# Row broadcasts of two heads in turn, and the first norm's sums from token-major squares

## The chip, the core and the metric

The kernel runs on one core of one Trainium2 chip, in one launch. The metric is the device time of an execution in microseconds (us), smaller is better. The core has a matrix engine (TensorE, PE in the profile, with its weight loads as PEld), VectorE (DVE), ScalarE (ACT), GpSimd (POOL) and a sync engine (SP) that issues most loads. Each engine runs its own instructions in order and waits on semaphores for the others.

## The reference

Two transformer blocks follow each other on 512 tokens of 1024 features, all in float32. Cut to what matters here:

```python
def first_block(x, ...):
    h = rmsnorm(x, norm1_g)                    # x * rsqrt(mean(x*x) + eps) * g, per token
    q, k, v, cb, cc, cx, g_attn, g_conv = split(h @ w_in)
    q, k = partial_rope(rmsnorm(q)), partial_rope(rmsnorm(k))     # per head of 64
    attn = windowed_gqa(q, k, v, sink)         # softmax over a window, 8 heads, 2 kv heads
    x = x + (sigmoid(g_attn) * (attn @ w_ap) + sigmoid(g_conv) * (conv @ w_cp)) @ w_out
    return x + hierarchical_moe(rmsnorm(x, norm2_g), ...)
def second_block(x, ...):
    # layer 0: two full attentions of 8 heads each ("a", and "b" from latents), then an MLP
    # layer 1: neighbourhood attention of 16 heads, then an MLP; a last norm
```

In each attention the output of a head is divided, per token, by the sum of its exponentials. In each norm the features are multiplied, per token, by the reciprocal root of the mean square.

## The kernel before

Activations lie feature-major: a tile has 128 features on the partitions and the 512 tokens along the row, and `x` is eight such tiles. Float32 products are made of three matmuls on split operands (`mm3`, L226 to L228: high by high, high by low, low by high), each of 512 tokens. Weights arrive in a ring of three buffers (`raw`, L103), are split by ScalarE (`wh`, L124) and VectorE (`wl`, L133) three groups ahead of their use, and a product of 8 blocks (24 matmuls) fills one of two accumulators (`psacc`).

The order of the instructions is written by generators. `run` steps a main generator, one quantum for each block of three matmuls, and lets a side generator (an attention) step in between; `later(n, f)` calls `f` after n quanta. So a number in `later` sets where in each engine's order an instruction stands, and not when it runs.

The start (`window`) loads `x` as `xin`, splits it into H and L, and makes products at once; the norm's factor is applied behind them. The first 16 quanta make the first two products block by block in turn; the third to sixth follow, 8 quanta each. `Heads.take` evicts each of the first five on ScalarE twice, scaled (`z`, L567) and squared (L568), and lets TensorE sum the squares per head four quanta on (`psO`, L300); the rotary part takes a shuffle on VectorE (L576), two multiplications on GpSimd (L577, L578) and an addition on VectorE (L582), and `write_q` casts the result on ScalarE (L640, L642). The sixth product is V (L626, transposed at L631).

The first norm's sum of squares is made beside this: `square` takes the eight tiles of `xin` in turns on ScalarE (L351, L357) and VectorE (L355), GpSimd adds them up in `ss` (L364), `norm_tokens` sums over the partitions with four matmuls (psT, L300), VectorE makes the factor `rcol` per token (L319 to L289), and `rows` broadcasts it along the partitions (`rstd`, L326, L333).

A row broadcast turns a column of 128 token values into a row that is the same on all partitions: the matmul takes the column, repeated, as the weights and the identity as the moving operand. Where two heads of 64 features share a tile, head 0 fills partitions 0 to 63 of the result and head 1 partitions 64 to 127, with 64 output columns each. This stands in `scale_k` (L611, the factor of k) and in `f_step` (L719, the reciprocal sums `rs` of the two heads of a unit; ScalarE copies the result to `rb`, L721). There are 4 units in the window attention, 4 and 4 in layer 0, and 8 in layer 1, where `GridPV` has its own `rows` with five pieces, the last of 64 tokens (L1410).

## Time and profile before

| | us |
| --- | --- |
| median of 3 runs | 1891.06 (1889.78 to 1893.31) |
| the profiled execution | 1888.91 |
| its span, first to last instruction | 1887.1 |
| TensorE busy in the span | 1824.1 |
| VectorE busy | 1080.7 |
| ScalarE busy | 724.4 |
| GpSimd busy | 342.3 |

The profile is of one execution. A matmul on float32 operands shows as two passes, and matmuls are pipelined, so the busy time of an engine is that in which at least one instruction was in flight. The stages by time: the window block to about 290 us, routing and experts to about 640, layer 0 to about 1320 with its attentions between 690 and 900, layer 1 from there with its attention between 1320 and 1500, then the last MLP. The clock of a row is the share of TensorE's full clock of 2.4 GHz that was granted on average over the stretch; the two levels are 1.2 and 2.4 GHz.

### The profile page before, as it was taken

Reading aid. Unit: us, or ns where it says so; the run is one execution under the profiler, and the core shown is the slowest. Engines: PE = TensorE matmul, PEld = TensorE weight load, DVE = VectorE, ACT = ScalarE, POOL = GpSimd, SP = SyncE. Lnnn points to the kernel's source line nnn. Section 1 sums busy time; section 2 is a strip of 40 time slices with the busy share of each in tenths; the row PEclk is TensorE's granted clock in tenths of the full one; section 3 lists DMA queues with packets and bytes.
Section 4 is the critical chain, followed back from the end, with each engine's and each line's share of the span. In section 5 each row is a group of like instructions: output and inputs, shape, how many; then the busy total and the mean of one; then the engine's idle time right before and its main releaser. Section 6 shows DMA issues by size and latency. Waiting matters only on the chain.

```text
span 1887.1 us, 23667 instructions
## 1 busy us (share of the span) xinstructions
PE 1824.1 (97%) x8890; PEld 1369.5 (73%) x8890; DVE 1080.7 (57%) x1956; ACT 724.4 (38%) x1418; POOL 342.3 (18%) x356
## 2 busy tenths in 40 slices
PE   7999999799999899999999999999999999999998
PEld 6777787534444686667888888878777788888887
DVE  7765447534433767765655555563766565555555
ACT  4444334211111456654433333333555443333334
POOL 5310003110000251001211111121443221111111
PEclk9999999899999999999999999999999999999999
DMA  5211336599999220302222222233222232322321
GB/s 189 77 51 68 131 131 252 183 359 417 422 419 403 88 95 18 84 29 84 101 101 89 102 100 89 102 128 117 79 57 57 90 112 90 107 95 90 107 94 45
DMA packets 67334, 257.08 MB, mean 136 GB/s; under 512 B 22224, under 2 KB 28752, under 8 KB 42128
## 3 DMA queue, kind: packets, MB, share of 16 engines
q1 hardware_dynamic: 54848, 227.41, 32.6%
q0 software_dynamic: 5712, 19.66, 3.2%
q10 hardware_dynamic: 6656, 8.45, 1.3%
q8 instruction: 72, 1.18, 0.3%
q14 instruction: 46, 0.38, 0.1%
HBM read 245.28 MB, written 8.39 MB: 134 GB/s over the span
## 4 chain that ended last, share of the span: by engine, by line
PE 56%; DVE 6%; ACT 2%; issue 1%; DMA 0%; POOL 0%; POOLq 0%; DVEq 0%; ACTq 0%
PE psacc L226 15%; PE psacc L228 15%; PE psacc L227 14%; PE psT L695 2%; PE psO L849 2%; DVE wl L133 1%; PE psT L326 1%; PE psO L1418 1%; PE psT L1410 1%; PE psS L1475 1%; PE psS L226 1%; PE psS L1159 1%; PE psS L227 1%; PE psS L228 1%; ACT p L682 1%
## 5 line engine op out<-in xcount | busy, mean ns | idle before, releaser
L133 DVE TENSOR_TENSOR wl<-raw,wh 128x512 fp32r<-128x512 f32 x466 | 403.3, 869 | 245.8 <-ACT wh L124 241.8
L226 PE MATMUL psacc<-xh,wh 128*128 128x512 f32 x1008 | 408.9, 406 | 7.0 <-ACT wh L124 6.4
L124 ACT CAST wh<-raw 128x512 fp32r<-128x512 f32 x466 | 285.8, 617 | 323.4 <-PE psacc L227 273.6
L227 PE MATMUL psacc<-xl,wh 128*128 128x512 f32 x1008 | 395.6, 392 | 1.2 <-DVE xl L250 1.2
L228 PE MATMUL psacc<-xh,wl 128*128 128x512 f32 x1008 | 395.9, 393 | 0.1
L226 PEld LDWEIGHTS psacc<-xh,wh 128*128 128x128 f32 x1008 | 190.9, 189 | 56.4 <-issue 14.2
L228 PEld LDWEIGHTS psacc<-xh,wl 128*128 128x128 f32 x1008 | 190.4, 189 | 41.9 <-DVE wl L133 0.6
L227 PEld LDWEIGHTS psacc<-xl,wh 128*128 128x128 f32 x1008 | 191.2, 190 | 35.4 <-DVE xl L250 2.5
L226 PE MATMUL psacc<-uh,wh 128*128 128x512 f32 x480 | 187.0, 390 | 2.6 <-DVE x L438 2.6
L228 PE MATMUL psacc<-uh,wl 128*128 128x512 f32 x480 | 186.8, 389 | 0.0
L227 PE MATMUL psacc<-ul,wh 128*128 128x512 f32 x480 | 186.7, 389 | 0.0
L406 POOL TENSOR_TENSOR t<-t,rstd 128x512 f32<-128x512 f32 x64 | 83.1, 1299 | 526.4 <-ACT t L405 526.4
L438 DVE TENSOR_TENSOR x<-psacc,x 128x512 f32<-128x512 f32 x120 | 82.7, 689 | 125.4 <-PE psacc L228 125.4
L364 POOL TENSOR_TENSOR ss<-ss,t 128x512 f32<-128x512 f32 (+1 forms) x56 | 69.6, 1242 | 262.0 <-ACT t L357 241.4
L226 PEld LDWEIGHTS psacc<-uh,wh 128*128 128x128 f32 x480 | 90.1, 188 | 22.3 <-issue 3.7
L228 PEld LDWEIGHTS psacc<-uh,wl 128*128 128x128 f32 x480 | 90.1, 188 | 18.9
L227 PEld LDWEIGHTS psacc<-ul,wh 128*128 128x128 f32 x480 | 90.1, 188 | 18.6
L242 ACT CAST uh<-t 128x512 fp32r<-128x512 f32 x64 | 39.7, 620 | 131.4 <-DVE t L407 131.4
L695 PE MATMUL psT<-cst,p 128*128 128x128 f32 x448 | 77.1, 277 | 13.1 <-ACT p L682 12.8
L695 PEld LDWEIGHTS psT<-cst,p 128*128 128x128 f32 x448 | 55.2, 140 | 42.4 <-ACT p L682 22.7
L405 ACT ACTIVATE t<-psacc 128x512 f32<-128x512 f32 x64 | 38.2, 597 | 80.7 <-PE psacc L228 80.7
L703 DVE COPY pt<-psT 128x256 f32<-128x256 f32 (+1 forms) x80 | 43.2, 540 | 39.4 <-PE psT L695 38.7
(461 smaller groups left out, 2786.1 us busy)
## 6 DMA issues: line engine op xcount, KB each, us to landing
raw<-ffn SPq DMA_DIRECT2D x64, 1024.0 KB, 4.8
ew<-e_w SPq DMA_DIRECT2D x15, 2048.0 KB, 11.2
raw<-e_w SPq DMA_DIRECT2D x20, 1024.0 KB, 10.0
esH<-e_w SPq DMA_DIRECT2D x8, 2048.0 KB, 12.8
esL<-e_w SPq DMA_DIRECT2D x8, 2048.0 KB, 12.5
raw<-w_in_a SPq DMA_DIRECT2D x8, 1024.0 KB, 4.8
raw<-od_qk SPq DMA_DIRECT2D x8, 1024.0 KB, 4.7
raw<-w_gccp SPq DMA_DIRECT2D x8, 768.0 KB, 4.1
```

The costliest lines, as they stand in the source:

```text
L124: nc.scalar.copy(h[:, :n], r)
L133: self.nc.vector.tensor_sub(l, r, h)
L226: nc.tensor.matmul(acc, wh, xh, start=first, stop=False)
L227: nc.tensor.matmul(acc, wh, xl, start=False, stop=False)
L228: nc.tensor.matmul(acc, wl, xh, start=False, stop=last)
L242: nc.scalar.copy(h, src)
L364: self.nc.gpsimd.tensor_add(s, s, q)
L405: nc.scalar.activation(r, acc, AF.Relu)
L406: nc.gpsimd.tensor_mul(r2, r, st["r2"])
L438: nc.vector.tensor_add(X[:, d], acc, X[:, d])
L695: nc.tensor.transpose(t[:, o:o + 128], p[:, m * 128:m * 128 + 128], c.ident)
L703: nc.vector.tensor_copy(dst, src)
```

## The change

First, `pair_rows` takes the place of the two calls of `rows` in `scale_k` and `f_step`: for each block of tokens it issues the matmul of head 0 and then that of head 1, and not all blocks of head 0 first. The five pieces of `GridPV` become a table that `pair_rows` reads. The matmuls themselves are the same.

Second, the first norm's sums come from another copy of `x`. The host lays out `xN`, with the tokens on the partitions (128 partitions, four tokens each, 1024 features a token). Three loads on SP's queue, behind the masks of the attention and ahead of the next weights, bring it into the three buffers `pt0` to `pt2`, which the attention uses only later. ScalarE squares eight pieces of 512 in place and sums each along the row (`accum_out`) into a column of `sq`. VectorE adds the two columns of a token, and the factor follows as before. The squares stand at quanta 25 to 39, where those of `xin` stood at 10 to 31; `stats` moves from 24 to 27 and `rows` from 31 to 33 quanta behind the second product. The squares of `xin`, the additions on GpSimd and the four matmuls over `ss` are gone.

```diff
-    def rows(self, cols, t, p0=0, p1=128):
+    def rows(self, cols, t):
...
+    def pair_rows(self, cols, t, pieces=None):
...
+        for i, o, a, n in pieces or [(i, i * 128, 0, 128) for i in range(cols.shape[1])]:
+            for h in range(2):
+                self.nc.tensor.matmul(t[64 * h:64 * h + 64, o:o + n], cols[:, i, h:h + 1].to_broadcast([128, 64]),
+                                      self.ident[:, a:a + n], start=True, stop=True)
...
-            for h in range(2):
-                c.rows(f[:, :, h], t, 64 * h, 64 * h + 64)
+            c.pair_rows(f, t)
...
-        for hh in range(2):
-            pv.rows(d["rs"][:, :, hh], t, 64 * hh, 64 * hh + 64)
+        c.pair_rows(d["rs"], t, pv.pieces)
...
-        c.later(10 + 3 * d, lambda d=d: c.square(s, xin[:, d], d, d % 2))
...
+    sq = pool.tile([128, 8], F32, name="sq")
+    for i, r in enumerate(room):
+        n = min(1536, 4096 - 1536 * i)
+        r = r.rearrange("p a b -> p (a b)")
+        nc.sync.dma_start(r[:, :n], a["xN"][:, 1536 * i:1536 * i + n])
+        for j in range(n // 512):
+            x, o = r[:, 512 * j:512 * j + 512], sq[:, 3 * i + j:3 * i + j + 1]
+            c.later(25 + 2 * (3 * i + j), lambda x=x, o=o: nc.scalar.activation(x, x, AF.Square, accum_out=o))
...
-        st["rcol"] = c.norm_tokens(s)
+        s4 = c.few((4,))
+        nc.vector.tensor_add(s4, sq[:, 0::2], sq[:, 1::2])
+        st["rcol"] = c.rstd(s4, 4, D)
...
-                c.later(24, stats)
-                c.later(31, rows)
+                c.later(27, stats)
+                c.later(33, rows)
```

How the order on GpSimd changes, from its first operation on 512 tokens to the start of the factors' chain; before:

```order
L364 TENSOR_TENSOR ss_90<-ss_90,t_219 128x512
L364 TENSOR_TENSOR ss_90<-ss_90,t_232 128x512
L577 TENSOR_TENSOR t_256<-z_235,wcos_152 128x512
L578 TENSOR_TENSOR t_257<-t_257,wsin_153 128x512
L577 TENSOR_TENSOR t_261<-z_239,wcos_152 128x512
L578 TENSOR_TENSOR t_262<-t_262,wsin_153 128x512
L364 TENSOR_TENSOR ss_90<-ss_90,t_269 128x512
L364 TENSOR_TENSOR ss_90<-ss_90,t_293 128x512
L364 TENSOR_TENSOR ss_90<-ss_90,t_316 128x512
L577 TENSOR_TENSOR t_325<-z_305,wcos_152 128x512
L578 TENSOR_TENSOR t_326<-t_326,wsin_153 128x512
```

and now (`z` are the evicted products, two multiplications for each):

```order
L591 TENSOR_TENSOR t_252<-z_231,wcos_151 128x512
L592 TENSOR_TENSOR t_253<-t_253,wsin_152 128x512
L591 TENSOR_TENSOR t_257<-z_235,wcos_151 128x512
L592 TENSOR_TENSOR t_258<-t_258,wsin_152 128x512
L591 TENSOR_TENSOR t_313<-z_295,wcos_151 128x512
L592 TENSOR_TENSOR t_314<-t_314,wsin_152 128x512
```

The additions into `ss` are gone, and the multiplications of the next product follow at once.

On ScalarE, from the square of the third product (its eviction `psacc`) to the weight cast behind the eviction of the fourth; before:

```order
L568 ACTIVATE t_306<-psacc_243 128x512
L124 CAST wh_310<-raw_113 128x512
L642 CAST qst_146<-z_239 64x512
L357 ACTIVATE t_336<-xin_91 128x512
L124 CAST wh_344<-raw_113 128x512
L640 CAST qst_146<-z_305 64x512
L567 ACTIVATE z_365<-psacc_309,gains_80 128x512
L568 ACTIVATE t_366<-psacc_309 128x512
L124 CAST wh_370<-raw_113 128x512
```

and now (`pt0` and `pt1` hold the copy of `x`):

```order
L582 ACTIVATE t_296<-psacc_239 128x512
L124 CAST wh_300<-raw_112 128x512
L908 ACTIVATE pt0_158,sq_161<-pt0_158 128x512
L655 CAST qst_145<-z_235 64x512
L908 ACTIVATE pt0_158,sq_161<-pt0_158 128x512
L124 CAST wh_330<-raw_112 128x512
L908 ACTIVATE pt0_158,sq_161<-pt0_158 128x512
L908 ACTIVATE pt1_159,sq_161<-pt1_159 128x512
L653 CAST qst_145<-z_295 64x512
L581 ACTIVATE z_350<-psacc_299,gains_80 128x512
L582 ACTIVATE t_351<-psacc_299 128x512
L124 CAST wh_355<-raw_112 128x512
```

One square of `xin` stood between the two evictions; now four squares of the copy stand there, and four more between the next two.

On TensorE, one broadcast of layer 1 with its neighbours; before:

```order
L226 MATMUL psacc<-xh,wh 128x512
L227 MATMUL psacc<-xl,wh 128x512
L228 MATMUL psacc<-xh,wl 128x512
L1410 MATMUL psT<-cst,rs 64x128 x3
L1410 MATMUL psT<-cst,rs 64x64 x2
L1410 MATMUL psT<-cst,rs 64x128 x3
L1410 MATMUL psT<-cst,rs 64x64 x2
L695 MATMUL psT<-cst,p 128x128 x2
```

and now:

```order
L226 MATMUL psacc<-xh,wh 128x512
L227 MATMUL psacc<-xl,wh 128x512
L228 MATMUL psacc<-xh,wl 128x512
L340 MATMUL psT<-cst,rs 64x128 x6
L340 MATMUL psT<-cst,rs 64x64 x4
L708 MATMUL psT<-cst,p 128x128 x2
```

The five pieces of head 0 stood ahead of the five of head 1; now each piece stands for both heads in turn.

## Rows read from the trace of the kernel before

**Rows 1.** The page: busy time, share of the span and instructions of each engine.
```profile
PE 1824.1 (97%) x8890; PEld 1369.5 (73%) x8890; DVE 1080.7 (57%) x1956; ACT 724.4 (38%) x1418; POOL 342.3 (18%) x356
```
**Rows 2.** Line views of L326 and L1410: duration ns min/median/max, first and last start, forms.
```profile
L326 PE MATMUL psT<-cst,rs x192: 272/273/323, 103.7 to 876.3; 128*64 128x128 f32 x192
...
L326 PE MATMUL psT<-cst,f x32: 272/273/323, 67.6 to 698.2; 128*64 128x128 f32 x32
...
L1410 PE MATMUL psT<-cst,rs x160: 219/272/323, 1346.8 to 1488.4; 128*64 128x128 f32 x96, 128*64 128x64 f32 x64
```
**Rows 3.** Timeline, TensorE: start, us, line, count of passes, [idle before <- releaser].
```profile
54.77 1.05 PE L326 MATMUL psT<-cst,rcol 128*128 128x128 f32 x8
...
103.68 1.58 PE L326 MATMUL psT<-cst,rs 128*64 128x128 f32 x16
...
103.68 1.34 PEld L326 LDWEIGHTS psT<-cst,rs 128*64 128x64 f32 x16 [0.36 <-issue]
...
109.31 0.65 PE L820 MATMUL psO<-pt,V 128*64 128x256 f32 x4
...
1370.93 1.81 PE L1410 MATMUL psT<-cst,rs 128*64 128x128 f32 x20
```
**Rows 4.** L326 in two stretches: us, PE busy (x in flight), PEld, PEclk, DMA, GB/s.
```profile
103.85:104.15 0.30, 0.30 (x4) 0.30 (x4) 1.00 0.94 369
104.19:104.49 0.30, 0.30 (x8) 0.30 (x8) 1.00 0.97 410
```
**Rows 5.** Waits of ScalarE, 690 to 900 and 1320 to 1500 us: total, times, longest.
```profile
ACT t L721 <- PE psT L326: 9.0, 6, 2.5
...
ACT t L721 <- PE psT L1410: 11.0, 7, 2.7
```
**Rows 6.** Timeline, TensorE, 20 to 52 us.
```profile
20.95 0.50 PE L226 MATMUL psacc<-xh,wh 128*128 128x512 f32 x1 [0.58 <-ACT t L568]
...
33.00 1.05 PE L300 MATMUL psO<-cst,t 128*128 128x2 f32 x8 [1.76 <-ACT t L568]
...
42.76 1.05 PE L300 MATMUL psO<-cst,t 128*128 128x2 f32 x8 [1.53 <-ACT t L568]
...
48.11 0.95 PE L300 MATMUL psT<-cst,ss 128*128 128x1 f32 x8
48.92 0.49 PE L226 MATMUL psacc<-xh,wh 128*128 128x512 f32 x1
...
51.79 0.95 PE L300 MATMUL psO<-cst,t 128*128 128x2 f32 x8
```
**Rows 7.** Timeline, ScalarE, 31 to 35 us.
```profile
31.26 0.62 ACT L640 CAST qst<-z 64x512 fp32r<-64x512 f32 x1 [5.78 <-DVE z L582]
...
34.12 0.63 ACT L357 ACTIVATE t<-xin 128x512 f32<-128x512 f32 x1
```
**Rows 8.** Timeline, VectorE and GpSimd, 19 to 33 us.
```profile
19.03 0.69 DVE L133 TENSOR_TENSOR wl<-raw,wh 128x512 fp32r<-128x512 f32 x1
...
27.75 3.48 DVE L582 TENSOR_TENSOR z<-t 128x512 f32<-128x512 f32 x2
...
27.24 1.74 POOL L578 TENSOR_TENSOR t<-t,wsin 128x512 f32<-128x512 f32 x1
28.94 3.41 POOL L364 TENSOR_TENSOR ss<-ss,t 128x512 f32<-128x512 f32 x2
```
**Rows 9.** Two stretches: us, PE, PEld, DVE, ACT, POOL busy (x), PEclk, DMA, GB/s.
```profile
33.00:38.50 5.50, 5.50 (x21) 4.54 (x22) 5.41 (x6) 2.21 (x4) 5.46 (x4) 0.69 0.00 0
...
42.70:48.10 5.40, 5.34 (x20) 4.42 (x21) 4.70 (x6) 1.81 (x5) 2.81 (x2) 0.68 0.48 182
```
**Rows 10.** Timeline, ScalarE, 708 to 710 us: exponentials that also sum their row.
```profile
708.83 0.78 ACT L682 ACTIVATE p<-psS,nm,fq 128x512 f32<-128x512 f32 x1 [0.53 <-DVE nm L1145]
...
709.67 0.78 ACT L682 ACTIVATE p<-psS,nm,fq 128x512 f32<-128x512 f32 x1
```
**Rows 11.** A stretch without loads: columns as in rows 9.
```profile
28.00:44.00 16.00, 12.71 (x56) 9.99 (x55) 14.61 (x13) 6.87 (x13) 14.14 (x9) 0.89 0.00 0
```

More of the change, by code (lines that the diff above doesn't have):

```diff
@@ L317, in norm_tokens, with rstd @@
             m = 4
+        return self.rstd(t[:, :m], m, n)
+    def rstd(self, t, m, n):
         a = self.few((m,))
-        self.nc.vector.tensor_scalar(a, t[:, :m], 1.0 / n, EPS, op0=OP.mult, op1=OP.add)
+        self.nc.vector.tensor_scalar(a, t, 1.0 / n, EPS, op0=OP.mult, op1=OP.add)
         r = self.tmp.tile([128, 4], F32, name="rcol", tag="rcol", bufs=3)[:, :m]
         return self.rsqrt(a, (m,), r)
-    def rows(self, cols, t, p0=0, p1=128):
+    def rows(self, cols, t):
         for i in range(cols.shape[1]):
-            self.nc.tensor.matmul(t[p0:p1, i * 128:i * 128 + 128], cols[:, i:i + 1].to_broadcast([128, p1 - p0]),
+            self.nc.tensor.matmul(t[:, i * 128:i * 128 + 128], cols[:, i:i + 1].to_broadcast([128, 128]),
                                   self.ident, start=True, stop=True)
+    def pair_rows(self, cols, t, pieces=None):
[3 more added lines that the diff above has]
+                                      self.ident[:, a:a + n], start=True, stop=True)
     def row_tile(self, cols):
@@ L796, in __init__ @@
         self.ready = True
+    pieces = None
     def order(self, i, m):
         return m
-    def rows(self, *args):
-        self.c.rows(*args)
     def kbs(self, i):
@@ L858, in window @@
     c.mark("win")
-    H, L, s, _ = c.norm_begin(GAINS["norm1"])
+    H = c.slab.tile([128, NB, T], F32R, name="xh", tag="H")
+    L = c.slab.tile([128, NB, T], F32R, name="xl", tag="L")
     xin = c.xs.tile([128, NB, T], F32, name="xin", tag="X")
@@ L1405, in dst @@
         return pt[:, 4 * i - 2:4 * i + 2] if i < 3 else pt[:, 10:12]
-    def rows(self, cols, t, p0, p1):
-        nc, c = self.c.nc, self.c
-        for i, o, a, n in ((0, 64, 0, 128), (1, 192, 0, 128), (2, 320, 0, 128), (3, 0, 64, 64), (3, 448, 0, 64)):
-            nc.tensor.matmul(t[p0:p1, o:o + n], cols[:, i:i + 1].to_broadcast([128, p1 - p0]),
-                             c.ident[:, a:a + n], start=True, stop=True)
+    pieces = ((0, 64, 0, 128), (1, 192, 0, 128), (2, 320, 0, 128), (3, 0, 64, 64), (3, 448, 0, 64))
     def run(self, u, pt, o):
@@ L2122, in lay_window @@
     o["xT"] = xT
+    o["xN"] = i["x"][0].reshape(4, 128, 1024).transpose(1, 0, 2).reshape(128, 4096)
     o["xP"] = perm(xT)
```

## Prediction

> **What bounds the kernel now.** I read the page first. TensorE is busy for 97% of the span [rows 1], so only two sorts of change can move the end: TensorE work that gets shorter, and the few places where TensorE stands still or runs at its lower clock. The next view is the group of the matmuls that the change rewrites. The row broadcasts with 64 output columns are 192 + 32 passes on one line and 160 on another [rows 2]; each fp32 matmul appears as two passes, so that is 12 + 2 broadcasts of 16 passes and 8 of 20. Third, the waits and the clock of the first 60 us: TensorE stands still for 1.76 and 1.53 us before the sums of squared head outputs (psO, L300) [rows 6], and after each of the two stalls stands a stretch with a granted clock of 0.69 and 0.68 [rows 9], that is, of pieces at 1.2 and pieces at 2.4 GHz. The shorter idle time of 0.58 us at 20.95 [rows 6] has no such stretch behind it.
>
> **Part 1, the broadcasts.** Before, the eight passes of head 0 stand ahead of the eight of head 1. What a reader must see is that the two column halves can work at once. In 0.30 us ahead of the middle of one broadcast 4 matmuls are in flight, and in the 0.30 us in the middle, where the tail of head 0 meets the start of head 1, 8 matmuls and 8 weight loads [rows 4]. So for a third of the way the halves already overlap, at the full pace of each, and the rest runs on one half. The whole takes 1.58 us [rows 3]. With the heads in turn the two streams begin together, and the end is that of one stream of eight passes. The nearest row for that is the eight-pass broadcast at full width, 1.05 us [rows 3]; the first pass of a 64-wide broadcast lasts up to 323 ns instead of 272 [rows 2], which adds 0.05. So one costs 1.05 to 1.10 us and saves 0.48 to 0.53; I take 0.49.
>
> For the 20-pass kind a half has six passes of 128 tokens and four of 64. The pitch of the first sort is (1.05 - 0.27) / 7 = 0.11 us; that of the second I estimate at half, since it streams half the tokens. One stream: 0.05 + 6 x 0.11 + 3 x 0.055 + 0.22 (the shortest pass [rows 2]) = 1.10 us. Before it takes 1.81 [rows 3], so 0.71 is saved; I take 0.70. Sum: 14 x 0.49 + 8 x 0.70 = 6.9 + 5.6 = 12.5 us.
>
> How much of it reaches the end? The window stage (five broadcasts, 2.5 us) is a row of products on TensorE, where it counts whole. In the two later attention stages (4.4 + 5.6 = 10.0 us) TensorE sometimes waits for exponentials, so a shorter broadcast could turn into a longer wait. Against that: ScalarE itself stands still until these broadcasts are done, 9.0 and 11.0 us in those stages [rows 5], with the next exponentials queued behind its copy, so it comes earlier too. I take 9.0 of the 10.0. Part 1 gives 11.5 us; the bounds are 2.5 (all lost there) and 12.5.
>
> The row in the middle of the broadcast is also where a rule of the notes can be weighed. The Trainium skill (TensorE: Matmul & The Clock Gate, Part 3: Packing small matmuls — row/col tiling) says that a weight load overlaps with matmuls in flight only when the row group differs. The two heads use the same 128 rows, so by that rule the halves would run one after the other and part 1 would be worth nothing; the 8 loads within 0.30 us [rows 4] speak against it. It is the first rival below.
>
> **Part 2, the first norm.** Removed: four ScalarE and four VectorE squares, seven GpSimd additions, and four matmuls that sum over features. The latter cost TensorE 48.92 - 48.11 = 0.81 us [rows 6]. Added: three loads of 2 MB in all, eight ScalarE squares with a sum, one small VectorE addition. The order of all engines behind the first 60 us stays as it was, apart from the broadcasts.
>
> Why did TensorE stall? Its psO sums wait for the eviction of the product before by L568 [rows 6]; that stands on ScalarE behind the cast L640, which waited 5.78 us for VectorE's addition L582 [rows 7]. VectorE's tensor-tensor operations there last 1.74 us each, while the same size takes 0.69 us when GpSimd does not run [rows 8], and GpSimd ran without a pause. The first four rotary products stand on GpSimd as before and end at 27.24 + 1.74 = 28.98; then it runs the norm's additions [rows 8]. Without these the second L582 finds VectorE free (the square ahead of it is gone) and GpSimd idle, and ends near 28.98 + 0.1 + 0.69 = 29.75 instead of 31.23. So the eviction and the psO sums come 1.48 us earlier: of the stall of 1.76 us about 0.3 is left.
>
> From there on ScalarE is the question, since all eight squares lie now within two products. Its own work per product is 34.12 - 31.26 = 2.86 us for five instructions [rows 7] and a second weight cast, 0.55 as a fifth of these. A square with its sum has no row; its nearest is the exponential with a sum at the same size, whose pitch is 709.67 - 708.83 = 0.84 us [rows 10] (bounds: 0.63 as a plain square [rows 7], 0.98 if nothing of the read of the sum overlaps). Four of them: 3.4. Together 6.8 us. TensorE takes 51.79 - 48.92 = 2.87 us for 12 matmuls, so 5.7 for a product, and 0.81 for its sums [rows 6], 6.5 us. ScalarE is behind by 0.3 us a product, up to 0.9 if a square costs 0.98: I allow 0.2 us of the second stall (1.53 - 0.2 = 1.3 gained), 0.3 for a new one at the third psO sums, and 0.3 for the transposes of V, whose copy is queued behind a cast that waits for the longer VectorE chain of the norm.
>
> Clock: the two stretches of 5.50 and 5.40 us at 0.69 and 0.68 lose (1 - 0.69) x 5.5 + (1 - 0.68) x 5.4 = 3.4 us [rows 9]. With stalls of 0.2 to 0.3 us instead I take it that they go, as after 20.95. Sum: 0.81 + 1.48 + 1.3 - 0.6 + 3.4 = 6.4 us; bounds: 0 (stalls and low clock stay, now from ScalarE's queue, and the 0.81 is spent) and 7.5 (no stall at all).
>
> The loads: on SP's queue they stand behind the masks and ahead of one weight load of 1 MB, and from 28 to 44 us nothing moves [rows 11]. 2.1 MB at 369 GB/s [rows 4] are 5.7 us, so that weight load lands near 28 + 5.7 = 34 us, in the empty stretch, and no product of the next 20 us uses it. The pieces land ahead of it, the last near 34 - 2.8 = 31 us, the first (0.8 of 2.1 MB) 3.6 us earlier. The first square stands behind the eviction that ends near 33.0 - 1.5 = 31.5, so it is covered by 4 us; if that cover were gone, every eviction would wait behind the square. The four matmuls that broadcast rcol move to behind the last product, at the same cost.
>
> **The sum.** 11.5 + 6.4 = 17.9 us. The profiled execution has 1888.91 us (span 1887.1), 2.15 below the median of the runs shown; the forecast for the median is 1891.06 - 17.9 = 1873.2, say 1873.
>
> **Rivals.** (a) The halves don't overlap better than now, or the later stages swallow it: part 1 gives nothing, only part 2 is left, 1891.06 - 6.4 = 1884.7. For it: waits for exponentials follow many broadcasts. Against: the 8 matmuls in flight [rows 4], and the products with V, which already go in turn: four passes of 256 tokens take 0.65 us [rows 3], and one after the other, at twice the pitch of 0.11, the last would only start at 0.66.
> (b) ScalarE is the new bound at the start: psO sums wait as before and the clock drops again. Part 2 gives 0, part 1 stays: 1891.06 - 11.5 = 1879.6. For it: 6.8 against 6.5 us per product; if a square costs 0.98 it is 7.4.
> (c) Slower: each change of the half drains the array. The nearest price is the 0.36 us that the weight loads stand still between full-width work and a broadcast [rows 3]. A 16-pass broadcast changes the half 7 times, a 20-pass one 9 times, 14 x 7 + 8 x 9 = 170 in all. The far end is 170 x 0.36 = 61 us; at a quarter of it, 15 us, the time is 1891.06 + 15 - 6.4 = 1900. It decides from (6.4 + 3.8) / 170 = 0.06 us a change on. Against it stand the same four passes.
> (d) It does not do what it says: the reordering is absorbed and ScalarE eats part 2: 1891, no change.
>
> **How the numbers follow.** Forecast 0.70, (a) 0.09, (b) 0.13, (c) 0.03, (d) 0.05. The forecast's own range goes from 1891.06 - 12.5 - 7.5 - 2 (the spread of the runs) = 1869 to some 1878; with (b) to 1882. (a), (c) and (d) stay out, 0.17. A difference of 0.2% (3.8 us) is about what a measurement of this kernel can tell from no change: faster 0.70 + 0.09 + 0.13 = 0.92, same 0.05, slower 0.03.
>
> **What would show it.** Right: the 16-pass broadcasts last about 1.09 us and the 20-pass ones 1.10; no idle time over 0.6 us before psO sums; granted clock 1.00 from 33 to 48 us; everything behind the last of the first products 6 us earlier; ScalarE's wait for broadcasts falls by about 0.5 us each. Wrong: broadcasts still at 1.5 us; TensorE's wait for ScalarE's exponentials grows by as much as the broadcasts shrink; a first square that waits for its load; a stretch with a clock near 0.7 that starts after the squares.

## The result and the profile after

| | before | after |
| --- | --- | --- |
| median | 1890.51 us (4 runs, 1889.78 to 1893.31) | 1875.02 us (4 runs, 1873.13 to 1875.69) |
| profiled execution, and its span | 1888.91, 1887.1 | 1875.47, 1873.7 |
| start of the first broadcast of `f` | 67.6 | 63.3 |
| start of the last broadcast of layer 1 | 1486.8 | 1473.7 |

The changed kernel is faster: the ratio of its time to that of before is 0.9914, 95% interval 0.9897 to 0.9931. The difference of the medians is 15.5 us; the prediction said 17.9 (1873.2 us, range 1869 to 1882). So the sign, the range and the order of size were right and 2.4 us are missing. They are looked for below by where each term sits: the start up to the first broadcast of `f`, and everything behind it.

First the broadcasts, as rows 2 and 3 showed them for the kernel before: the line's largest group (duration in ns min/median/max, first and last start, forms), and two places of the timeline.

```profile
L340 PE MATMUL psT<-cst,rs x352: 219/273/323, 98.8 to 1474.6; 128*64 128x128 f32 x144, 128*64 128x64 f32 x32
```

```profile
98.85 1.09 PE L340 MATMUL psT<-cst,rs 128*64 128x128 f32 x16
...
1460.37 1.11 PE L340 MATMUL psT<-cst,rs 128*64 128x128 f32 x20
```

A single pass is as long as before (273 ns, 219 for the shortest), but the whole broadcast takes 1.09 and 1.11 us where it took 1.58 and 1.81 [rows 3]: the prediction had 1.09 and 1.10. ScalarE's wait for them in layer 0 and in layer 1 follows (total us, times, longest; two windows, 690 to 900 and 1320 to 1500 us):

```profile
ACT t L733 <- PE psT L340: 6.1, 6, 2.0
...
ACT t L733 <- PE psT L340: 6.1, 5, 2.0
```

In layer 0 that is 6.1 us in 6 waits, and was 9.0 in 6 [rows 5], so 0.48 us less each. And the wait that part 1 could have turned into, TensorE's for the exponentials, did not grow. It was 5.1 us in nine waits and 6.3 us in six before (the first two lines), and is the same now (the last two; the two windows again):

```profile
PE psT L695 <- ACT p L682: 5.1, 9, 1.0
...
PE psT L695 <- ACT p L682: 6.3, 6, 1.6
```

```profile
PE psT L708 <- ACT p L695: 5.1, 9, 1.0
...
PE psT L708 <- ACT p L695: 6.3, 6, 1.6
```

Another wait for ScalarE did grow in layer 0, that for its copy of a broadcast, from 0.2 to 0.6 us; e1 below shows the place.

Now the start. The first view has the columns of rows 9; the second is the waits of TensorE between 31 and 59 us.

```profile
33.00:38.50 5.50, 5.50 (x25) 4.30 (x24) 4.44 (x7) 4.57 (x12) 1.88 (x2) 1.00 0.00 0
...
42.70:48.10 5.40, 5.14 (x27) 4.06 (x26) 3.76 (x9) 3.76 (x8) 1.50 (x3) 1.00 0.32 134
48.10:59.00 10.90, 9.20 (x46) 7.20 (x45) 8.61 (x21) 3.85 (x7) 3.30 (x6) 1.00 0.26 86
```

```profile
PE psO L300 <- ACT t L582: 1.4, 3, 1.0
PE psT L644 <- ACT t L639: 1.3, 1, 1.3
PE psT L330 <- DVE rcol L289: 0.4, 1, 0.4
```

The half clock of 0.69 and 0.68 [rows 9] is gone, as foreseen. The stalls are smaller but not gone: 0.95, 0.19 and 0.26 us ahead of the sums of squared head outputs (psO), and 1.32 us at the transposes of V, which had 0.2. In the last stretch TensorE is busy for 9.20 of 10.90 us.

So at the first broadcast of `f` the gain was 4.3 us and not 6.4. From there to the end it is 13.4 - 4.3 = 9.1 us, where 11.5 were expected. The experiments take the two apart.

### The profile page after: what moved, and what is told of

The parts are those of the page before. It is cut to its first block, busy times and chain, and to the rows that moved or that the text cites. A ratio compares the mean times of both kernels' runs of the same rounds, so it can differ in the third digit from the quotient of the medians.

```text
span 1873.7 us, 23657 instructions
## 1 busy us (share of the span) xinstructions
PE 1812.2 (97%) x8882; PEld 1355.7 (72%) x8882; DVE 1072.9 (57%) x1953; ACT 727.3 (39%) x1430; POOL 329.8 (18%) x349
## 3 DMA queue, kind: packets, MB, share of 16 engines
q8 instruction: 72, 1.18, 0.3%
## 4 chain that ended last, share of the span: by engine, by line
PE 56%; DVE 6%; ACT 3%; issue 1%; DMA 0%; POOL 0%; POOLq 0%; DVEq 0%; ACTq 0%
PE psacc L226 15%; PE psacc L228 15%; PE psacc L227 15%; PE psT L708 2%; PE psO L860 2%; DVE wl L133 1%; PE psT L340 1%; PE psO L1435 1%; PE psS L226 1%; PE psS L1180 1%; PE psS L1492 1%; PE psS L227 1%; PE psS L228 1%; ACT p L695 1%; ACT wh L124 1%
## 5 line engine op out<-in xcount | busy, mean ns | idle before, releaser
L124 ACT CAST wh<-raw 128x512 fp32r<-128x512 f32 x466 | 285.6, 617 | 321.9 <-PE psacc L227 272.5
L228 PEld LDWEIGHTS psacc<-uh,wl 128*128 128x128 f32 x480 | 90.1, 188 | 18.8
L378 POOL TENSOR_TENSOR ss<-ss,t 128x512 f32<-128x512 f32 (+1 forms) x49 | 58.5, 1195 | 240.2 <-ACT t L371 239.9
L248 DVE TENSOR_TENSOR ul<-t,uh 128x512 fp32r<-128x512 f32 x64 | 44.3, 693 | 35.6 <-ACT uh L242 34.4
## 6 DMA issues: line engine op xcount, KB each, us to landing
ew<-e_w SPq DMA_DIRECT2D x15, 2048.0 KB, 11.8
```

The costliest lines, as they stand in the source:

```text
L124: nc.scalar.copy(h[:, :n], r)
L228: nc.tensor.matmul(acc, wl, xh, start=False, stop=last)
L248: nc.vector.tensor_sub(l, src, h)
L378: self.nc.gpsimd.tensor_add(s, s, q)
```

## Experiments

All profiles in one table. Starts are read from the trace of each; "last two" is the time from the start of the last but one broadcast of layer 1 to that of the last, which the theory of one term needs. The times of the kernel before beside e1 to e3 and e8 were 1890.02 us, beside a2 and e4 to e6 1889.44, beside e7, e9 and e10 1889.38, beside e12 1889.40.

| kernel | what | first `f` | last two | span | median |
| --- | --- | --- | --- | --- | --- |
| before | | 67.59 | 12.50 | 1887.1 | 1890.51 |
| e1 | before + pairs | 69.10 | 11.78 | 1877.2 | 1878.19 |
| e3 | before, sums late | 68.81 | 12.50 | 1889.5 | 1889.82 |
| e7 | before, addition late | 65.01 | 14.05 | 1886.2 | 1887.09 |
| e8 | before, no GpSimd additions | 63.21 | 12.49 | 1883.6 | 1886.84 |
| e2 | after, heads one behind the other | 62.44 | 14.08 | 1883.7 | 1883.06 |
| after | | 63.32 | 13.36 | 1873.7 | 1875.02 |
| a2 | after again | 62.74 | 13.34 | 1871.9 | 1873.95 |
| e4 | after, no squares | 63.15 | 13.35 | 1872.0 | 1873.78 |
| e6 | after, heads change every two | 63.34 | 13.12 | 1872.9 | 1874.92 |
| e5 | after, sums, V and factor's broadcast late | 61.69 | 13.32 | 1869.6 | 1872.17 |
| e9 | after, addition late | 60.27 | 13.30 | 1867.1 | 1870.88 |
| e10 | e9 + sums, V and factor late | 59.79 | 13.34 | 1869.3 | 1870.90 |
| e12 | e10, factor early again | 58.77 | 13.34 | 1866.4 | 1870.16 |

A single profile is no measure of the total to better than some 2 us: the stretch from the fifth broadcast to the sixth (routing and experts, where only one broadcast lies) took between 484.3 and 488.2 us in these fourteen. So totals are taken from medians, and single profiles are read by stage.

### The two parts alone

Part 1 alone (e1) is the kernel before with this and the table of pieces:

```diff
-            for h in range(2):
-                c.rows(f[:, :, h], t, 64 * h, 64 * h + 64)
+            c.pair_rows(f, t)
...
-        for hh in range(2):
-            pv.rows(d["rs"][:, :, hh], t, 64 * hh, 64 * hh + 64)
+        c.pair_rows(d["rs"], t, pv.pieces)
```

> The kernel before with the broadcasts of two heads in turn and nothing else. Theory: the two parts add up. Each 16-pass broadcast falls by 0.49 us and each 20-pass one by 0.70, and the changed kernel's gain of 15.5 us less the 4.3 us that its first 64 us gave leaves 11.2 us: 1890.5 - 11.2 = 1879.3, with the first broadcast of f still at 67.6 us. Rival 1: all 12.5 us reach the end, and the 0.9 us that the changed kernel lost near 1468 us was an accident of that kernel: 1878.0. Rival 2: the later stages swallow more when the start is not also earlier: a gain of 9 us or less, 1881.5 or more.

Measured: 1878.19 us, ratio 0.9937 (0.9924 to 0.9951), a gain of 11.8 us; the prediction's term was 11.5. Rival 1 (1878.0) is the nearest by the number, but the theory's 1879.3 lies within the interval too (1875.7 to 1880.8). In the profile the last broadcast of layer 1 starts 9.73 us earlier than before and the first of `f` 1.51 us later, 11.2 us between them. The gain grows from each broadcast to the next by 0.49 us and then by 0.70. Two are lost: one in layer 0, and, as far as one profile tells, most of the last one of layer 1 (the span ends 9.92 us earlier, only 0.2 more). The one in layer 0 turned into a longer wait for ScalarE. ScalarE comes to its copy of that broadcast only behind a row of casts and an exponential, in which it never stands still, and the second group of TensorE's transposes behind the broadcast waits for the copy, 0.15 us before and 0.64 us in e1 (start, us, ... [idle before <- releaser]):

```profile
774.32 0.66 PE L695 MATMUL psT<-cst,p 128*128 128x128 f32 x4 [0.15 <-ACT t L721]
```

```profile
771.91 0.66 PE L704 MATMUL psT<-cst,p 128*128 128x128 f32 x4 [0.64 <-ACT t L729]
```

Part 2 alone (e2) is the changed kernel with the two loops of `pair_rows` swapped:

```diff
-        for i, o, a, n in pieces or [(i, i * 128, 0, 128) for i in range(cols.shape[1])]:
-            for h in range(2):
+        for h in range(2):
+            for i, o, a, n in pieces or [(i, i * 128, 0, 128) for i in range(cols.shape[1])]:
```

> The changed kernel with the matmuls of each broadcast back in the old order, all of head 0 and then all of head 1. Theory: only the new norm is left, and it is worth what the first 64 us of the changed kernel's profile showed, 4.3 us: 1890.5 - 4.3 = 1886.2, with the first broadcast of f at 63.3 us. Rival: the prediction's 6.4 us, of which 2 us are hidden in the changed kernel by chance on VectorE and GpSimd: 1884.1. The broadcasts should last 1.58 and 1.81 us again.

Measured: 1883.06 us, ratio 0.9962 (0.9949 to 0.9976), a gain of 7.0 us; the first broadcast of `f` came at 62.44 us and not at 63.3, and the broadcasts last 1.58 and 1.81 us again. The rival's 1884.1 was nearer than the 1886.2 of the theory. So the 4.3 us of the first pair of profiles was a poor measure: the old start reached that broadcast at 67.59, 69.10 and 68.81 us in three profiles (before, e1, e3), the new one at 63.32, 62.44, 62.74 and 63.34 (after, e2, a2, e6). The means are 68.5 and 63.0, and the difference 5.5 us. The 7.0 us may flatter part 2 in turn. Three of e2's five executions had a mean granted clock of 0.991, which none of the twenty of the kernel before beside it reached (0.987 to 0.990). The other two had 0.989 and took 1884.44 and 1885.53 us, 5.6 and 4.5 us below the kernel before. Only one of these two was profiled, so where the three ran at the higher clock is not known.

### What paced the start

The prediction priced two stalls and two stretches at half clock, one by one. The test is to take the first stall away without taking any work away: the kernel before with the sums later (e3). The condition picks the heads of the first attention, at the start.

```diff
-        c.later(4, sums)
+        c.later(7 if self.mask == WSWAP else 4, sums)
```

> The kernel before with one number changed: the sums of squared head outputs at the start stand seven instead of four quanta behind their product. No work is taken away. Theory: the two stalls of 1.76 and 1.53 us are what costs the start its time, first as idle time and then by the half clock behind them; three quanta are 2.1 us, so both stalls go and the granted clock stays at 1.00 from 33 to 48 us: 3.3 + 3.4 = 6.7 us at most, some of it back at other waits, 1884 to 1886.5. Rival: the late eviction is waited for in another place anyway (the next product or the column sums), and under 1.5 us is gained: 1889 or more.

Measured: 1889.82 us, ratio 1.000 (0.9991 to 1.0009). Nothing was gained. The rows say why. Here are ScalarE's casts of the rotated heads (`qst<-z`) and TensorE's sums, first of e1, whose start is the old one unaltered, then of e3 (start, us, ... [idle before <- releaser]):

```profile
31.25 0.62 ACT L649 CAST qst<-z 64x512 fp32r<-64x512 f32 x1 [6.29 <-DVE z L592]
41.05 0.62 ACT L649 CAST qst<-z 64x512 fp32r<-64x512 f32 x1 [5.80 <-DVE z L592]
48.06 0.62 ACT L649 CAST qst<-z 64x512 fp32r<-64x512 f32 x1 [3.54 <-DVE z L592]
...
32.99 1.05 PE L300 MATMUL psO<-cst,t 128*128 128x2 f32 x8 [2.27 <-ACT t L578]
42.79 1.87 PE L300 MATMUL psO<-cst,t 128*128 128x2 f32 x8 [3.15 <-ACT t L578]
```

```profile
31.80 0.62 ACT L640 CAST qst<-z 64x512 fp32r<-64x512 f32 x1 [4.24 <-DVE z L582]
41.62 0.62 ACT L640 CAST qst<-z 64x512 fp32r<-64x512 f32 x1 [5.83 <-DVE z L582]
48.62 0.62 ACT L640 CAST qst<-z 64x512 fp32r<-64x512 f32 x1 [3.52 <-DVE z L582]
...
33.53 1.05 PE L300 MATMUL psO<-cst,t 128*128 128x2 f32 x8 [0.22 <-ACT t L568]
43.36 1.76 PE L300 MATMUL psO<-cst,t 128*128 128x2 f32 x8 [3.18 <-ACT t L568]
```

The casts are 9.80 and 7.01 us apart in e1 and 9.82 and 7.00 in e3. In the kernel before they stand at 31.26 [rows 7], 41.02 and 48.04, so 9.76 and 7.02. That does not depend on what TensorE does. The eviction of the next product stands behind each cast on ScalarE, and the cast waits for VectorE's addition (L582). What holds the addition up is VectorE's own queue. Here is VectorE in the kernel before:

```profile
37.03 1.66 DVE L133 TENSOR_TENSOR wl<-raw,wh 128x512 fp32r<-128x512 f32 x1
38.61 1.78 DVE L355 TENSOR_TENSOR t<-xin 128x512 f32<-128x512 f32 x1
40.31 0.68 DVE L582 TENSOR_TENSOR z<-t 128x512 f32<-128x512 f32 x1
...
43.25 1.10 DVE L133 TENSOR_TENSOR wl<-raw,wh 128x512 fp32r<-128x512 f32 x1 [0.58 <-ACT wh L124]
```

GpSimd's products for the addition at 40.31 were done at 38.14. But from the end of one addition (31.23 us) to the end of the next (40.99) VectorE has no pause over 0.04 us, and four of its operations in between last 1.66 to 1.78 us each beside GpSimd. In the second step a loop closes: VectorE waits for a weight cast (L124), which stands on ScalarE behind the eviction, which stands behind the cast of the heads, which waits for the addition. Both are called the chain below. TensorE's stalls are its slack. In e3 the first stall is 0.22 us instead of 1.76, and the second 3.18 instead of 1.53.

The same rows price the clock. The stretch from 33 to 38.5 us in e1 (columns as in rows 9), and that from 42.7 us:

```profile
33.00:38.50 5.50, 5.50 (x28) 4.71 (x29) 5.41 (x6) 2.20 (x4) 5.47 (x4) 1.00 0.00 0
...
42.70:48.10 5.40, 5.31 (x17) 4.54 (x18) 4.69 (x6) 1.81 (x5) 2.83 (x2) 0.50 0.49 165
```

e1 had the full clock from 33 to 38.5 us, the kernel before 0.69 [rows 9]. It reached the sums 1.6 us earlier, waited 3.15 us instead of 1.53, and went on at 42.79 instead of 42.76. The clock in that stretch was worth nothing. In the next stretch it was worth something, because there no wait for a cast followed: 0.50 instead of 0.68 over 5.4 us are 1.0 us, and the first broadcast of `f` came 1.5 us later. e3 had the full clock up to 42.7 us, 0.58 from there to 48.1 and 0.74 from there to 59. Its third cast came no earlier for the full clock, and `f` came 1.2 us later than in the kernel before, 0.5 of it already in the first cast.

What shortens the chain? The kernel before without the additions of the norm on GpSimd (e8) leaves ScalarE's and VectorE's squares and the column sums in place:

```diff
-            self.nc.gpsimd.tensor_add(s, s, q)
+            if add:
+                self.nc.gpsimd.tensor_add(s, s, q)
```

> The kernel before without the seven GpSimd additions of the first norm: the squares are still made on ScalarE and VectorE, but only the first of the eight tiles is in the sum, so that part of the computation is left out. Theory: the VectorE additions of the rotary part were slow because GpSimd ran beside them, and stood late behind it; without the additions the first stall falls from 1.76 to 0.3 to 1.0 us, the second below 0.5, and the half clock goes: a gain of 3.5 to 6 us, 1884.5 to 1887. Rival: the squares on VectorE and ScalarE are what delays the evictions: the first stall stays above 1.4 us and the gain is under 1.5 us, 1889 or more.

Measured: 1886.84 us, ratio 0.998 (0.997 to 0.9989), so 3.2 us, just under the theory's 3.5 to 6. The first broadcast of `f` came at 63.21 us, against 68.5 on average with the additions. The second stall is gone. The first is still 1.18 us, more than the theory said, and the half clock stayed behind it (0.69 from 33 to 38.5 us), so what was gained there was not gained by the clock. Its casts:

```profile
30.14 0.62 ACT L641 CAST qst<-z 64x512 fp32r<-64x512 f32 x1 [5.20 <-DVE z L583]
37.55 0.62 ACT L641 CAST qst<-z 64x512 fp32r<-64x512 f32 x1 [3.41 <-DVE z L583]
44.39 0.62 ACT L641 CAST qst<-z 64x512 fp32r<-64x512 f32 x1 [3.36 <-DVE z L583]
```

They are 7.41 and 6.84 us apart, and in the changed kernel 6.84 and 6.89. So the additions were what made the first step long. By its one profile nearly all of part 2's gain at the start comes from them (5.3 of 5.5 us); by the medians it is 3.2 of e2's 7.0 us, and the two intervals (2.1 to 5.7 us and 4.5 to 9.6) only just overlap. How much of part 2 the additions are is not settled closer.

The other way to break the chain is to leave all work and let the addition and the cast stand three quanta later, behind the next eviction (e7):

```diff
-            c.later(5, lambda: add(t1, t2))
+            c.later(8 if self.mask == WSWAP else 5, lambda: add(t1, t2))
```

> The kernel before with one number changed: the rotary addition of a head (VectorE) and the cast behind it (ScalarE) stand eight instead of five quanta behind the rotary products, so that on ScalarE the eviction of the next product stands ahead of that cast and not behind it. GpSimd's additions, the squares and the column sums all stay. Theory: the start of the kernel before was bound by the chain eviction, rotary products on GpSimd, addition, cast, next eviction, and TensorE's stalls and half clock were its slack; with the eviction ahead of the cast the first broadcast of f comes 3.5 to 5.5 us earlier (67.6, 68.8 and 69.1 us in three profiles of the old start) and the kernel gains as much: 1884.5 to 1886.5. Rival: GpSimd and VectorE have no room for it, the evictions keep their times, and it is as with the later column sums: within 1.5 us of 1889.5.

Measured: 1887.09 us, ratio 0.9987 (0.9978 to 0.9996), a gain of 2.3 us, and `f` at 65.01 us. That is between theory and rival. The one number that moves the cast gains where the one that moves the sums gained nothing, so it is the chain that counts; but one stall of 1.96 us stays, since VectorE and GpSimd, each slowed by the other, deliver the additions late even then. Its profile also has the stretch at half clock near the end of layer 1 (1.6 us, last section), which the other profiles of the old start do not have.

### Is ScalarE the new bound?

Rival (b) of the prediction, tested by the changed kernel without its eight squares (e4):

```diff
-            c.later(25 + 2 * (3 * i + j), lambda x=x, o=o: nc.scalar.activation(x, x, AF.Square, accum_out=o))
+            pass
```

> The changed kernel without the eight squares on ScalarE: the sums of squares are a constant, so that part of the computation is left out; loads, factor and all other steps stay. Theory: a square takes 0.63 to 0.72 us and ScalarE has slack for four a product, so nothing is gained beyond the waits of 0.3 us before the sums: within 1 us of the changed kernel, with the first broadcast of f at 62.4 to 63.3 us. Rival, the prediction's case that ScalarE is the new bound at the start: the evictions come 1 to 2 us earlier for the third and fourth product and the kernel gains as much, 1.5 us or more.

Measured: 1873.78 us, against 1873.95 for the changed kernel beside it (a2). The squares cost nothing that can be measured. In the changed kernel ScalarE even waits behind them:

```profile
34.86 0.63 ACT L908 ACTIVATE pt<-pt 128x512 f32<-128x512 f32 x1
...
35.48 0.62 ACT L908 ACTIVATE pt<-pt 128x512 f32<-128x512 f32 x1
...
37.08 0.62 ACT L653 CAST qst<-z 64x512 fp32r<-64x512 f32 x1 [0.89 <-DVE z L596]
```

From one square to the next it is 0.62 us, with the read of the sum (0.18 us) in it, and ScalarE then stands still for 0.89 us until VectorE releases the cast. The prediction took 0.84 from the exponentials, its lower bound was 0.63.

### Are changes of the half free?

The heads in turn change the half of the array seven times in a 16-pass broadcast. With a change every two matmuls it is three times (e6):

```diff
+        ps = pieces or [(i, i * 128, 0, 128) for i in range(cols.shape[1])]
+        for b in range(0, len(ps), 2):
+            for h in range(2):
+                for i, o, a, n in ps[b:b + 2]:
```

> The changed kernel with the heads changing every two matmuls (four passes) instead of every one. Before, with one change in the middle, the first to the last start of a 16-pass broadcast took 1.31 us; in turn, with seven changes, 0.82. Theory: a change costs nothing, each half is a stream of its own, and what counts is how far behind its neighbour the other half starts; with three changes a broadcast takes 0.85 to 1.0 us and the kernel loses 0 to 3 us. Rival, a part of the drain per change that the prediction set as its slower case: with fewer changes the broadcast is shorter than 0.82 us and the kernel gains.

Measured: 1874.92 us, against 1873.95 (a2), within the spread of both. The broadcasts take 1.14 and 1.16 us:

```profile
98.92 1.14 PE L342 MATMUL psT<-cst,rs 128*64 128x128 f32 x16
...
1360.06 1.16 PE L342 MATMUL psT<-cst,rs 128*64 128x128 f32 x20
```

From the first start to the last it is 0.87 us, in turn 0.82, with one change 1.31. Fewer changes are not shorter, so rival (c) is out. And three changes already give nearly all. That fits two streams of which the later only has to get its first work early; this reading was not tested further.

### The changed kernel again, and its waits moved

> The changed kernel once more, unaltered, beside its variants and with a profile of its own. Two questions. First, the sum of the parts: the pairs alone gained 11.8 us and the norm alone 7.0, together 18.8, while the first comparison gave 15.5. Theory: the parts add up within the spread of the runs, and this one comes out at 1871.5 to 1875. Rival: they get in each other's way by some 3 us, and it is 1875 to 1876 again. Second, the stretch at half clock from 1468.6 to 1472.2 us behind a wait of 1.35 us: theory, it comes and goes with the execution, and a profile without it has 1.6 us less between the last two broadcasts (11.8 and not 13.4 us); rival, it belongs to this kernel and stands there again.

Measured: 1873.95 us, ratio 0.9923 (0.9909 to 0.9936), 15.5 us below the kernel before beside it. The gains of e1 and e2 add to 18.8, 3.3 us more; each has an interval of some 2.5 us to either side, so this is at the edge of what the runs can tell, and the clock of e2's executions may be a part of it. The profiles show no place where the parts disturb each other: from the first `f` to the end of the span a2 takes 1809.1 us, e1 1808.1, and 1.6 us of a2's are the stretch at half clock of which the last section tells. Single profiles differ by some 2 us there, so the 3.3 us stay open. On its second question the rival held: that stretch stood there again.

The casts of this profile, and of the first one of the changed kernel:

```profile
29.64 0.62 ACT L653 CAST qst<-z 64x512 fp32r<-64x512 f32 x1 [5.35 <-DVE z L596]
...
43.37 0.62 ACT L653 CAST qst<-z 64x512 fp32r<-64x512 f32 x1 [0.95 <-DVE z L596]
52.13 0.62 ACT L653 CAST qst<-z 64x512 fp32r<-64x512 f32 x1 [5.27 <-DVE z L596]
```

```profile
30.24 0.62 ACT L653 CAST qst<-z 64x512 fp32r<-64x512 f32 x1 [6.07 <-DVE z L596]
...
52.72 0.62 ACT L653 CAST qst<-z 64x512 fp32r<-64x512 f32 x1 [5.26 <-DVE z L596]
```

The whole chain starts 0.6 us earlier in a2, and its first stall is 0.24 us and not 0.95. The last cast comes 8.7 us behind the one before, in both: between them VectorE makes the factor `rcol` (2.9 us, from 47.70 to 50.64 in the first profile) ahead of the addition. V's copy is queued behind that cast, and so the transposes wait 1.3 us.

Three of TensorE's places later, no work changed (e5):

```diff
-        c.later(4, sums)
+        c.later(7 if self.mask == WSWAP else 4, sums)
...
-    c.later(2, turn)
+    c.later(5, turn)
...
-                c.later(33, rows)
+                c.later(36, rows)
```

> The changed kernel with three numbers moved: the sums of squared head outputs at the start seven instead of four quanta behind their product, the transposes of V five instead of two, the broadcast of rcol at 36 instead of 33 quanta. No work changes. In the profile of the changed kernel TensorE waits at these places for 1.4, 1.3 and 0.4 us. Theory: the chain on VectorE and GpSimd is no longer the bound of the start, so TensorE's own waits count, and 1.5 to 3 us are gained: 1.5 to 3 us below the changed kernel of this call. Rival: as with the same move in the kernel before, which gained nothing, the evictions keep their times and the waits come back in the next places: within 0.7 us.

Measured: 1872.17 us, 1.8 less than a2; the two ranges of runs overlap (1871.38 to 1873.72, and 1872.60 to 1875.32). By the number it is the theory, by the rows half of the rival: the waits ahead of the sums are gone, the casts keep their distances (30.57, 37.41, 44.32, 53.06), and the waits of 1.3 us for V and 0.4 for `rcol` are as long as before, since TensorE, no longer held up at the sums, comes there as early before the copy as it did, with three blocks more done.

Then the chain itself, with the edit of e7 in the changed kernel (e9):

> The same change of one number in the changed kernel. Theory: the evictions no longer wait for the rotary chain, so the waits ahead of the sums (0.7 to 1.4 us) go, and the copy of V, which stood behind the last of these casts, is early, so the wait of 1.3 us at the transposes goes too: 1.5 to 2.5 us less than the changed kernel, 1871.5 to 1872.5. Rival: the long chain of the norm's factor on VectorE then holds up TensorE in the same place (the broadcast of rcol, waited for 0.4 us now): under 0.8 us gained.

Measured: 1870.88 us, ratio 0.9906 (0.9891 to 0.9921), 18.5 us below the kernel before beside it, where a2 had 15.5. That is 3.1 us less than a2, where the theory said 1.5 to 2.5; the four runs lie between 1869.26 and 1872.38, so the excess is no more than their spread. The eviction now stands ahead of the cast:

```profile
35.52 0.67 ACT L581 ACTIVATE z<-psacc,gains 128x512 f32<-128x512 f32 x1
...
42.47 0.67 ACT L581 ACTIVATE z<-psacc,gains 128x512 f32<-128x512 f32 x1
45.67 0.62 ACT L653 CAST qst<-z 64x512 fp32r<-64x512 f32 x1 [1.54 <-DVE z L596]
```

The evictions are 6.95 us apart, and TensorE's waits between 30 and 60 us are 0.3 us for sums and 0.9 for `rcol`. The last two runs move that one. e10 puts the factor and everything that needs it later, e12 only what needs it:

```diff
-        c.later(4, sums)
+        c.later(5 if self.mask == WSWAP else 4, sums)
...
-    c.later(2, turn)
+    c.later(5 if late else 2, turn)
...
-                c.later(27, stats)
-                c.later(33, rows)
+                c.later(32, stats)
+                c.later(37, rows)
```

> The changed kernel with the addition and the cast late, the sums five quanta behind their product, the norm's factor five and its broadcast four quanta later, and the transposes of V three later. Theory: none of TensorE's waits between 30 and 55 us is left, 2.5 to 3.5 us less than the changed kernel in all: 1870.5 to 1871.5, with the first broadcast of f near 60 us. Rival: the waits return behind it, at the first products that need the factor: within 1 us of the variant with the late addition alone. For the stretch at half clock near the end of layer 1, which stood in all profiles of the new norm and in none of the old: if it is the norm's kernel that brings it, it stands here again (13.3 us between the last two broadcasts and not 11.8).

Measured: 1870.90 us, ratio 0.9903 (0.9888 to 0.9918): no better than e9, the wait for `rcol` is still 0.9 us.

> The variant before this one with the norm's factor back at 27 quanta behind the second product, and its broadcast kept at 37; all else as there (late addition and cast, sums at five, transposes of V at five). In that variant TensorE's only wait between 30 and 59 us that is left is the 0.9 us for rcol, since the factor's chain of 3 us on VectorE started four quanta ahead of the broadcast. Theory: with ten quanta between them that wait goes, the first broadcast of f comes at 58.9 us, and the kernel takes 0.9 us less, 1870.0. Rival: VectorE is the bound by now, the chain ahead pushes casts and weights behind it, and the wait returns at a product or at the transposes of V: no gain within 0.5 us. For the stretch at half clock near 1468 us, which came in nine of thirteen profiles: no expectation.

Measured: 1870.16 us, ratio 0.9900 (0.9884 to 0.9917). The wait is gone and `f` comes at 58.77 us, 1.0 earlier. This is the lowest median of the study, 19.2 us below the kernel before beside it, where the changed kernel was 15.5 below. The medians of e9, e10 and e12 lie within 0.7 us of each other, which four runs of each cannot tell apart.

## Why the prediction was right, and where it was not

- Part 1, 11.5 us: right, 11.8 in e1, and for the reason given. The lengths of 1.09 and 1.10 us were right to 0.01, the waits for exponentials did not grow, and a tenth of the later stages' 10 us is lost, as allowed; a half of that went into a longer wait for ScalarE's copy and not for exponentials. Rivals (a) and (c) are out. Sixteen passes start within 0.82 us, 0.055 apart, half the 0.11 us of one stream, and between 99.10 and 99.40 us 10 matmuls and 8 weight loads of a broadcast are in flight. The rule of the Trainium skill (TensorE: Matmul & The Clock Gate, Part 3: Packing small matmuls — row/col tiling) that a weight load overlaps with matmuls in flight only when the row group differs does not hold for these two column halves on the same rows, and the measurement decides.
- Part 2, 6.4 us: the sum holds (7.0 in e2; 5.5 at the first `f`), its terms do not. The step that failed is the pricing of the stalls (1.48 and 1.3) and of the clock (3.4) as costs of their own that add up. The old start was paced by the casts, 9.8 and 7.0 us apart; a stall that was removed came back at the next place (e3), and a full clock became a longer stall (e1). What part 2 did is shorten these steps to 6.8 and 6.9 us a product, and e8 has 7.4 and 6.8 with the GpSimd additions alone gone. That is near TensorE's own pace: in e9, where it hardly waits, the evictions are 6.95 us apart. Counted at the casts, from before to after, the first one comes 1.0 us earlier (the prediction's 1.48), the next step is 2.9 us shorter, the next 0.1, and the way from the third cast to `f` 0.2; this makes the 4.3. For all behind the first cast the prediction had 1.3 + 3.4 + 0.81 - 0.6 = 4.9. That the whole came near (6.4, and 5.5 on average) owes something to luck, since the clock term filled the place of the shorter step. The 0.81 for the column sums was not tested by itself.
- The 0.69 us of VectorE at 19.03 [rows 8] was read as its time without GpSimd. GpSimd ran from 19.27 on; VectorE had started first (last section). Without GpSimd it is the same 0.69, at 29.52 in the changed kernel.
- The first stall, 0.3 us left: 0.95 in the one profile, over the 0.6 that was to show the forecast right, and 0.24 in the other. The addition was put at 29.75 us and ended at 30.2 and 29.6.
- The second stall, 0.2: 0.19. The third, 0.3: 0.26.
- A square at 0.84 us: mis-sized, 0.62. ScalarE still had 0.9 us in hand in each product, so rival (b), at 0.13 the likeliest of the rivals, had less behind it than it was given.
- The transposes of V, 0.3: mis-sized, 1.3 us, the same in all six profiles of the new start with the early cast. The reason given was right (V's copy behind a cast that waits for the factor's chain), its length was not worked out: ten instructions, 2.9 us, of which one takes 1.18 while GpSimd runs.
- The loads covered: right. No square waited for one.
- Not in the prediction: 1.6 us near the end of layer 1 (last section).

Together: 11.8 for part 1 by the medians and 5.5 for the start by the profiles, less 1.6 there, are 15.7, and 15.5 were measured. By medians alone the parts are 18.8. Which of the two sums is right is not settled.

## What to carry to other kernels

Before stalls are added up, look for the engine or the chain that sets their period: if the same instruction on another engine comes at the same distance whatever the stalled engine does, the stalls and the clock are its slack, and only what shortens or reorders that chain pays. On an engine that works in order, an eviction that frees others should not stand behind an instruction that waits for the chain the eviction itself starts. Two streams like these, of 64 output columns each on different halves of the array, should be issued in turn, or at least in small groups.

## What was not expected of the hardware

- **Who goes first.** VectorE and GpSimd slowed each other when both ran on 512 tokens (VectorE 1.77 us instead of 0.69). Near 22.2 us both come to an operation, and GpSimd's waits for the load of the table `wcos`. In the first profile of the changed kernel that load took 5.7 us from issue to landing, and GpSimd was first:

```profile
22.21 1.29 POOL L591 TENSOR_TENSOR t<-z,wcos 128x512 f32<-128x512 f32 x1 [21.77 <-DMA wcos<-wcos]
...
22.28 1.77 DVE L133 TENSOR_TENSOR wl<-raw,wh 128x512 fp32r<-128x512 f32 x1 [3.38 <-ACT wh L124]
23.98 0.72 DVE L590 STREAM_SHUFFLE t<-z 128x512 f32<-128x512 f32 x1
```

  In the second (a2) it took 6.1 us, and VectorE was first:

```profile
22.40 0.69 DVE L133 TENSOR_TENSOR wl<-raw,wh 128x512 fp32r<-128x512 f32 x1 [3.38 <-ACT wh L124]
...
22.69 1.56 POOL L591 TENSOR_TENSOR t<-z,wcos 128x512 f32<-128x512 f32 x1 [22.25 <-DMA wcos<-wcos]
...
23.02 0.74 DVE L590 STREAM_SHUFFLE t<-z 128x512 f32<-128x512 f32 x1
```

  The shuffle comes 0.96 us earlier then, and the first cast 0.6. The Trainium skill (SBUF — State Buffer, SBUF: two separate sides) has it that VectorE, with two operands from SBUF, and GpSimd contend for one pair of ports, and that the one that starts first holds it for its whole instruction while the other waits. The two orders agree with that: the first one in lasts 1.29 and 0.69 us, the second 1.77 and 1.56. In the five profiles where the load took 6.0 or 6.1 us VectorE was first (e2, e7, e9, e12, a2); in the nine where it took 5.5 to 5.8, GpSimd, but for the kernel before, where VectorE led by 0.01 us. So some tenths of a microsecond at the start differ from execution to execution of one program with the landing of one load, and the first stall with them.
- **Half clock behind a wait, or not.** Near the end of layer 1's attention TensorE waits 1.35 us for attention outputs, in every profile. In ten of the fourteen a stretch at half clock follows, in four (before, e1, e3, e8) none. In the changed kernel (start, us, ...), and the clock of that stretch (columns as in rows 9):

```profile
1467.88 0.50 PE L226 MATMUL psacc<-oh,wh 128*128 128x512 f32 x1 [1.35 <-ACT oh L242]
1468.60 0.62 PE L227 MATMUL psacc<-ol,wh 128*128 128x512 f32 x1 [0.23 <-DVE ol L248]
1469.02 0.63 PE L228 MATMUL psacc<-oh,wl 128*128 128x512 f32 x1
1469.45 0.63 PE L226 MATMUL psacc<-oh,wh 128*128 128x512 f32 x1
```

```profile
1468.70:1472.00 3.30, 3.30 (x9) 2.51 (x10) 0.80 (x2) 0.29 (x2) 0.00 (x0) 0.52 0.02 5
```

  The matmuls start 0.43 us apart and not 0.23, which is the lower of the two levels, 1.2 GHz. It costs 1.6 us: the last two broadcasts are 13.36 us apart, in e1 11.78. It stood in all profiles of the new norm and in none of the old but e7's, so it is not the norm itself. What decides it was not found, and stays open.
